# Merged branches in buffers of their own, normed x kept, two more pairs by seven products, another opening: one edit of a two-layer encoder kernel on one core

## The chip, the cores and the metric

The kernel runs on one core of a Trainium2 chip. The metric is the device time of one execution in microseconds (us). The kernel before took 1723.2, 1725.94 and 1726.93 us in three runs, median 1725.94.

The core's engines work side by side, each through its own instructions in order: TensorE (PE) multiplies matrices into PSUM, VectorE (DVE) and ScalarE (ACT) do elementwise work, GpSimd (POOL) and SyncE (SP) here mostly issue DMAs. They wait for one another by semaphores.

## The reference

Two layers of an encoder trunk over x of 512 tokens by 1024 features, all in float32. Each layer normalizes x, projects it once for four token mixers and their gates, merges the gated mixers, adds an output projection to x, and then does the feed-forward part (FFN) that the change is about:

```python
for l in range(DEPTH):
    h = rmsnorm(x, ln_mix[l])
    z = h @ w_in[l]
    ...
    merged = jnp.zeros_like(x)
    for n, o_branch in enumerate((o_mla, o_fnet, o_diff, o_hgrn)):
        gate = jax.nn.sigmoid(gate_logits[..., n * D_MODEL:(n + 1) * D_MODEL].astype(jnp.float32))
        merged = merged + gate.astype(x.dtype) * (o_branch @ w_branch[l, n])
    x = x + merged @ w_out[l]

    h2 = rmsnorm(x, ln_ffn[l])
    g_part, u_part = jnp.split(h2 @ w_gate_up[l], 2, axis=-1)
    x = x + (jax.nn.silu(g_part) * u_part) @ w_down[l]
```

with `rmsnorm(x, g) = x * rsqrt(mean(x * x) + eps) * g` over the features. The FFN is 2816 wide: 22 tiles of 128 for g and as many for u.

## The kernel before

**Tiles.** x lies in SBUF as eight tiles of 128 features by 512 tokens (`xin`, later `xm`; `x[k]` in the code). A product in float32 precision is made from three matmuls in a reduced format: each operand is split into a high part (an ACT copy, L121 or, with a gain, L125) and a low part (DVE: source minus high part, L122 or L126), and `mm3` (L141 to L143) multiplies high by high, low by high and high by low. In the profile the names say which is which: `wr_` is a weight as loaded, `wh_` and `wl_` its parts; `hh..` and `hl..` are the parts of the activations; the letters behind name the use (`hf`, `hq`, `hg`: the first projections; `o`: output projection; `fr`: the first three FFN products; `f`: the other FFN tiles; `d`: the down projection). One `gemm` over 1024 features is 24 matmuls of 512 columns. Weights come through two buffers `wr` and three each of `wh` and `wl`.

**Norm.** `prenorm` splits x times the gain without waiting for the norm, sums the squares of x on ACT and DVE (`sq`, `ss`), has PE add over the partitions with a matrix of ones (`ssx`), and makes the scale r from it: Ln and Exp on ACT (L150, L151, tile `y`), three DVE steps (L152 to L154, `ya` and `r`). The first products use x that isn't scaled and are multiplied by r behind (`gs<-fr`, `us<-fr`); meanwhile `normed` writes the normalized x into the same `hh`, `hl` buffers for the products that follow.

**Output projection.** The merged branches are split into `mh`, `ml`, which take the buffers `hh`, `hl` of the pool hp; eight products `o` follow, each added to `x[nt]`.

**FFN.** 22 pairs j of a g tile and a u tile. The string `SEVEN` says how a pair is made. An 8 is an ordinary pair, two `gemm`s of 24 matmuls (`eight`, L1150); the first three products of pairs 0 and 1 (`fr0` to `fr2`) are made before r is there. A 7 (`seven`, L1119) makes the pair from seven products of half size in place of eight, Strassen's way: 84 matmuls of 256 columns, L1066, into `fa`, `fb`, `fc`. It needs sums of weight blocks (`sums`, L1069): SP loads `s31`, a GpSimd DMA adds other blocks onto it in flight, `a22` is loaded too, DVE adds `s24`, and all are split (`vh_f`, `vl_f`, `wh_f`, `wl_f`). It also needs sums of the normalized x, made once a layer in four steps (`right_sums`, behind pairs 0 to 3): `tt` and its parts `th`, `tl`. For these the normalized tile `xn` is computed a second time (`gained`, L1034). The `fr` tiles and `fb` share two PSUM banks, and the other products share four.

After 8, 16 and 22 pairs the down projection `d` adds its part to x.

**Order.** The order of the instructions on each engine is set by a scheduler that lists them by priority, its own estimates of time, and the buffers that are free. `tc.high_priority(AHEAD)` lets a weight's loads and splits run ahead of the code around them; `keep_in_program_order` holds an instruction where it is written. At run time each engine keeps to its list. The mixers are put in order by the string `ORDER`, which isn't touched.

## Time and profile before

| | us |
|---|---|
| three runs | 1723.2, 1725.94, 1726.93 (median 1725.94) |
| profiled execution | 1724.95 |
| its span, first to last instruction | 1723.2 |
| PE busy | 1697.8 (99%) |
| DVE busy | 1179.0 (68%) |
| ACT busy | 808.8 (47%) |
| POOL busy | 43.0 (2%) |

The page gives for each group of instructions the line, engine and operation, the tiles written and read, and the count; the views of the trace give start and duration of each instruction and, in brackets, how long its engine stood idle before it and what ended that. `SPq` marks a DMA issued by SP. Matmuls are pipelined: their rows overlap, so the time of one is read from the distance between starts.

The stages in the first layer by the trace: first products from 6.6 us, output projection from 467.4, FFN from 511.9, the first pair by seven products from 579.4; in the second layer the output projection begins at 1321.3 and the FFN at 1365.8.

### The profile page before, as it was taken

The page shows a single profiled execution, that of the slowest core. Times are in us where ns is not written, and L with a number is a line of the kernel's source. Part 1 is how long each engine was busy: PE and PEld are TensorE (multiplying, and loading weights), DVE is VectorE, ACT ScalarE, POOL GpSimd, SP SyncE. Part 2 cuts the span into 40 slices and gives each one's busy share as a digit, 9 for nine tenths or more (in the row PEclk, how much of TensorE's full clock was granted, in tenths as well). Part 3 has the DMA queues.
Part 4 walks back from the last instruction along what each step waited for, and adds up shares of the span by engine and source line. Part 5 has one row for each costly group of instructions (what it writes and reads, how often), then busy time and mean ns, then how long its engine had stood idle before and what let it go on. Part 6 is the DMA issues. An engine that isn't in the chain of part 4 may idle for free.

```text
span 1723.2 us, 25722 instructions
## 1 busy us (share of the span) xinstructions
PE 1697.8 (99%) x10220; PEld 1422.5 (83%) x10220; DVE 1179.0 (68%) x1979; ACT 808.8 (47%) x1352; POOL 43.0 (2%) x68
## 2 busy tenths in 40 slices
PE   8999999999999999999999999999999999999999
PEld 6787778877787989989887777788777788899897
DVE  8858775457769647748677687754667695487473
ACT  7374353456555424525453743534564453254251
POOL 1000000000000000000000000000000000000000
PEclk9999999999999999999999999999999999999999
DMA  5222203332262435644442221142323624365443
GB/s 193 64 80 86 74 26 115 105 99 86 87 201 100 138 110 161 170 122 126 133 136 58 87 74 62 43 119 97 110 75 111 189 87 140 118 177 145 127 115 104
DMA packets 62473, 191.58 MB, mean 111 GB/s; under 512 B 7953, under 2 KB 9361, under 8 KB 62353
## 3 DMA queue, kind: packets, MB, share of 16 engines
q1 hardware_dynamic: 56304, 170.10, 30.4%
q0 software_dynamic: 5760, 19.42, 6.2%
q8 instruction: 80, 1.31, 0.3%
q10 hardware_dynamic: 288, 0.43, 0.1%
q14 instruction: 41, 0.33, 0.1%
HBM read 179.42 MB, written 4.19 MB: 107 GB/s over the span
## 4 chain that ended last, share of the span: by engine, by line
PE 87%; DVE 7%; ACT 3%; DMA 2%; issue 1%; SPq 0%; POOLq 0%; ACTq 0%; DVEq 0%
PE fb L1066 8%; PE g L142 6%; PE g L141 6%; PE g L143 6%; PE fc L1066 5%; PE fa L1066 5%; PE d L141 5%; PE d L143 5%; PE d L142 5%; PE f L142 3%; PE f L141 3%; PE f L143 3%; DMA s_f<-in_w_gu 2%; PE av L942 1%; PE sm L909 1%; PE hf L142 1%
## 5 line engine op out<-in xcount | busy, mean ns | idle before, releaser
L141 PE MATMUL g<-hhm,wh_g 128*128 128x512 f32 x512 | 202.0, 394 | 0.0
L143 PE MATMUL g<-hhm,wl_g 128*128 128x512 f32 x512 | 201.5, 394 | 0.0
L142 PE MATMUL g<-hlm,wh_g 128*128 128x512 f32 x512 | 201.5, 394 | 0.0
L143 PE MATMUL d<-ah,wl_d 128*128 128x512 f32 x352 | 136.9, 390 | 0.5 <-DVE wl_d L122 0.5
L141 PE MATMUL d<-ah,wh_d 128*128 128x512 f32 x352 | 137.2, 392 | 0.0
L142 PE MATMUL d<-al,wh_d 128*128 128x512 f32 x352 | 137.1, 390 | 0.0
L122 DVE TENSOR_TENSOR wl_g<-wr_g,wh_g 128x1024 fp32r<-128x1024 f32 x64 | 78.3, 1223 | 73.8 <-ACT wh_g L121 73.8
L121 ACT ACTIVATE wh_g<-wr_g 128x1024 fp32r<-128x1024 f32 x64 | 67.7, 1058 | 115.4 <-PE g L142 80.1
L142 PEld LDWEIGHTS g<-hlm,wh_g 128*128 128x128 f32 x512 | 96.3, 188 | 20.4 <-issue 1.5
L141 PEld LDWEIGHTS g<-hhm,wh_g 128*128 128x128 f32 x512 | 96.3, 188 | 20.2 <-issue 0.8
L143 PEld LDWEIGHTS g<-hhm,wl_g 128*128 128x128 f32 x512 | 96.3, 188 | 20.0 <-issue 0.8
L121 ACT ACTIVATE wh_d<-wr_d 128x1024 fp32r<-128x1024 f32 (+1 forms) x48 | 47.5, 989 | 111.7 <-PE d L142 85.5
L118 DVE TENSOR_TENSOR xm<-xm,d 128x512 f32<-128x512 f32 x48 | 33.0, 688 | 88.9 <-PE d L143 88.8
L121 ACT ACTIVATE wh_f<-wr_f 128x1024 fp32r<-128x1024 f32 x50 | 53.0, 1059 | 79.1 <-PE d L142 35.0
L121 ACT ACTIVATE vh_f<-s_f 128x512 fp32r<-128x512 f32 x64 | 40.1, 630 | 103.4 <-PE fb L1066 63.8
L910 DVE TENSOR_REDUCE nm<-sm 128x1 f32<-128x512 f32 x64 | 43.8, 689 | 51.3 <-PE sm L909 50.9
L143 PEld LDWEIGHTS d<-ah,wl_d 128*128 128x128 f32 x352 | 66.1, 188 | 14.9 <-DVE wl_d L122 1.4
L141 PEld LDWEIGHTS d<-ah,wh_d 128*128 128x128 f32 x352 | 66.0, 188 | 14.9 <-ACT ah L121 1.9
L142 PEld LDWEIGHTS d<-al,wh_d 128*128 128x128 f32 x352 | 66.1, 188 | 14.0 <-DVE al L122 1.2
L1066 PE MATMUL fb<-th,vh_f 128*128 128x256 f32 x256 | 75.7, 296 | 0.4 <-DVE uu L118 0.3
L1066 PE MATMUL fa<-hhf,wl_f 128*128 128x256 f32 x256 | 72.7, 284 | 0.0
L1066 PE MATMUL fa<-hlf,wh_f 128*128 128x256 f32 x256 | 72.5, 283 | 0.0
(444 smaller groups left out, 4845.6 us busy)
## 6 DMA issues: line engine op xcount, KB each, us to landing
wr_g<-in_w_g SPq DMA_DIRECT2D x64, 512.0 KB, 3.6
wr_f<-in_w_gu SPq DMA_DIRECT2D x50, 512.0 KB, 3.5
s_f<-in_w_gu SPq DMA_DIRECT2D x32, 512.0 KB, 4.5
s_f<-in_w_gu POOLq DMA_DIRECT2D x32, 512.0 KB, 5.4
wr_d<-in_w_d SPq DMA_DIRECT2D x32, 512.0 KB, 3.5
wr_b<-in_w_b SPq DMA_DIRECT2D x16, 512.0 KB, 3.4
wr_o<-in_w_o SPq DMA_DIRECT2D x16, 512.0 KB, 3.5
a_f<-in_w_gu SPq DMA_DIRECT2D x32, 256.0 KB, 3.0
```

The lines of the kernel that those rows point to most:

```text
L118: V.tensor_tensor(out, a, b, op=ALU.add)
L121: A.activation(hi, src, AF.Copy)
L122: V.tensor_tensor(lo, src, hi.bitcast(F32), op=ALU.subtract)
L141: T.matmul(ps, lh, rh, start=first, stop=False)
L142: T.matmul(ps, lh, rl, start=False, stop=False)
L143: T.matmul(ps, ll, rh, start=False, stop=last)
L909: T.matmul(ps, qs[0:96, t * P:(t + 1) * P], ks[0:96], start=True, stop=True)
L910: V.tensor_reduce(nm[:, j:j + 1], ps, axis=AX.X, op=ALU.max, negate=True)
L942: T.matmul(av[e * 64:e * 64 + 64], vv[:, b, 2 * i + e], pts[i][e][:, b].rearrange("p t q -> p (t q)"), start=t == 1 and b == 0, stop=b == ...
L1066: T.matmul(ps[:, :H], lh[:, c], rh, start=first and k == 0 and n == 0, stop=k == Q - 1 and n == 2, skip_group_check=True)
```

## The change

There are four edits.

- *Opening.* The table of gains and constants (`pk`) is loaded and ACT's function table set before anything else; PE gets ten matmuls of a 128x128 tile of ones into a PSUM tile that nobody reads; the loads of x and of the first two weights keep the written order, with the second weight (hf01) in two halves between the tiles of x.
- *Merged branches.* `mh` and `ml` lie in a pool `om` that is open from the first merged tile to the last output product, and no longer in the buffers of `hh` and `hl`.
- *Normed x.* `normed` writes each `xn[k]` into a buffer of its own (those of the later `ah4` to `ah7` and `al4` to `al7`), and `right_sums` reads it there.
- *Pairs.* `SEVEN` has four 8s in place of six: pairs 4 and 5 of each layer are made by seven products.

```diff
--- before.py
+++ after.py
@@ -29,8 +29,9 @@
 LOG_EXP = "natural_log_exp_and_others"
 WL, WR = 3, 2
 LAYERS = range(L)
-SEVEN = "8888887777777777777777"
+SEVEN = "8888777777777777777777"
 AHEAD = 156
+EARLY = 10
 ORDER = "ccbccchhhchhcbchcghcchcchzccczccbccccccchgcgccchbbbcbhcgbzcbbcbccbgghcbgcgcbcccghchghchzhbccccbccccgcccccczhgcgbgchcgcccccccggggggbgcggggbcbbggcbbcbhcccbccbccccccccccccccccccbchccgbgggbchcbbbbbbhbbb"
 PE = 8
 PM = 4
@@ -74,10 +75,17 @@
             pool("pq", 2, space=bass.MemoryType.PSUM) as pq:
 
 
+        pk0 = cp.tile([P, PK_N], F32, tag="pk", name=f"pk{LAYERS[0]}")
+        tc.keep_in_program_order(nc.scalar.dma_start(pk0, io["pk"][LAYERS[0]]))
+        tc.keep_in_program_order(nc.scalar.preload_act_table_set(LOG_EXP))
+        ones = cl.tile([P, P], F32, name="ones")
+        V.memset(ones, 1.0)
+
+        early = pq.tile([P, S], F32, tag="sc", name="early")
+        for _ in range(EARLY):
+            T.matmul(early[:, :P], ones, ones, start=True, stop=True)
         ident = cl.tile([P, P], F32, name="ident")
         make_identity(nc, ident)
-        ones = cl.tile([P, P], F32, name="ones")
-        V.memset(ones, 1.0)
         blk64 = cp.tile([P, P], F32, name="blk64")
         V.memset(blk64, 0.0)
         V.memset(blk64[0:64, 0:64], 1.0)
@@ -89,11 +97,11 @@
         xpool = [None]
         x = []
 
-        def load_x(src, who):
+        def load_x(src, who, keep=lambda i: i):
             xpool[0] = pool(f"x{who}", side="right")
             px = xpool[0].__enter__()
             x[:] = [px.tile([P, S], F32, name=f"x{who}_{k}") for k in range(KD)]
-            return [lambda k=k: nc.sync.dma_start(x[k], src[k]) for k in range(KD)]
+            return [lambda k=k: keep(nc.sync.dma_start(x[k], src[k])) for k in range(KD)]
 
         def drop_x():
             xpool[0].__exit__(None, None, None)
@@ -125,13 +133,13 @@
             A.activation(hi, src, AF.Copy, scale=g)
             V.scalar_tensor_tensor(lo, src, g, hi.bitcast(F32), op0=ALU.mult, op1=ALU.subtract)
 
-        def weight(src, n, name, cuts=(), between=None):
+        def weight(src, n, name, cuts=(), between=None, keep=lambda i: i):
             raw = rp.tile([P, 1024], F32, tag="wr", name=f"wr_{name}")
             hi = wp.tile([P, 1024], F32R, tag="wh", name=f"wh_{name}")
             lo = wp.tile([P, 1024], F32R, tag="wl", name=f"wl_{name}")
             with tc.high_priority(AHEAD):
                 for a, b in zip((0,) + cuts, cuts + (n,)):
-                    nc.sync.dma_start(raw[:, a:b], src[:, a:b])
+                    keep(nc.sync.dma_start(raw[:, a:b], src[:, a:b]))
                     split(hi[:, a:b], lo[:, a:b], raw[:, a:b])
                     if between:
                         between.pop()()
@@ -226,25 +234,31 @@
         xs = nc.dram_tensor("x_mid", (KD, P, S), F32).ap()
         for l in LAYERS:
             lam_init = 0.8 - 0.6 * math.exp(-0.3 * l)
-            pk = cp.tile([P, PK_N], F32, tag="pk", name=f"pk{l}")
-            tc.keep_in_program_order(nc.scalar.preload_act_table_set(LOG_EXP))
-            nc.scalar.dma_start(pk, io["pk"][l])
+            if l == LAYERS[0]:
+                pk = pk0
+            else:
+                pk = cp.tile([P, PK_N], F32, tag="pk", name=f"pk{l}")
+                tc.keep_in_program_order(nc.scalar.preload_act_table_set(LOG_EXP))
+                nc.scalar.dma_start(pk, io["pk"][l])
 
 
             if l == LAYERS[0]:
                 with tc.high_priority(1000):
-                    loads = load_x(io["x"], "in")
-                    w0 = weight(io["w_z"][l, 0], 1024, "hf00", (256,), [loads[1], loads[0]])
-                    for load in loads[2:]:
-                        load()
+                    loads = load_x(io["x"], "in", tc.keep_in_program_order)
+                    some = lambda *ks: lambda: [loads[k]() for k in ks]
+                    w0 = weight(io["w_z"][l, 0], 1024, "hf00", (256,), [some(1, 2, 3), some(0)],
+                                tc.keep_in_program_order)
+                    w1 = weight(io["w_z"][l, 1], 1024, "hf01", (512,), [some(6, 7), some(4, 5)],
+                                tc.keep_in_program_order)
             else:
+                w1 = None
                 w0 = weight(io["w_z"][l, 0], 1024, "hf00")
             with pool(f"mo{l}") as mo, pool(f"mx{l}") as mp:
                 hh, hl, scale, normed = prenorm(pk[:, PK_MIX:PK_MIX + 8], f"m{l}")
                 first = [gemm(None, hh, hl, "hf00", w0)]
                 r = scale()
                 for c, name in ((1, "hf01"), (4, "hq0"), (6, "hg0")):
-                    first.append(gemm(io["w_z"][l, c], hh, hl, name))
+                    first.append(gemm(io["w_z"][l, c], hh, hl, name, w1 if c == 1 else None))
                 sig0 = mp.tile([P, 3, S], F32, name="sig0")
                 for j in range(2):
                     mul(sig0[:, j], first[j], r)
@@ -366,12 +380,16 @@
                         yield gate(n, nt)
                     done.add("gates")
 
-                mh, ml = [], []
+
+                mh, ml, om = [], [], []
 
                 def merged(n):
+                    if not om:
+                        om.append(pool(f"om{l}"))
+                        om.append(om[0].__enter__())
                     for k in range(len(mh), n):
-                        h = hp.tile([P, S], F32R, tag="hh", name=f"mh{k}", bufs=KD)
-                        lo = hp.tile([P, S], F32R, tag="hl", name=f"ml{k}", bufs=KD)
+                        h = om[1].tile([P, S], F32R, name=f"mh{k}")
+                        lo = om[1].tile([P, S], F32R, name=f"ml{k}")
                         split_g(h, lo, acc[k], 0.5)
                         mh.append(h)
                         ml.append(lo)
@@ -971,7 +989,7 @@
                             if t == NT - 1:
                                 yield f"b{2 * KD - 1}"
                                 yield from normed(i)
-                        done.add(2)
+                    done.add(2)
 
                 def chain(*gens):
                     for g in gens:
@@ -1012,6 +1030,7 @@
                 for nt in range(KD):
                     ps = gemm(io["w_o"][l, nt], mh, ml, f"o{nt}", wo.get(nt))
                     add(x[nt], x[nt], ps)
+                om[0].__exit__(None, None, None)
 
 
 
@@ -1029,18 +1048,20 @@
                 def minus_sub(out, a, b):
                     V.scalar_tensor_tensor(out, a, -1.0, b, op0=ALU.mult, op1=ALU.subtract)
 
-                def gained(k, r):
-                    xn = tmp([P, S], "sq", name="xn")
-                    V.scalar_tensor_tensor(xn, x[k], pk[:, PK_FFN + k:PK_FFN + k + 1], r, op0=ALU.mult, op1=ALU.mult)
-                    return xn
+                xn = {}
 
                 def normed(r):
+
                     for k in range(KD):
-                        split(hh[k], hl[k], gained(k, r))
-
-                def right_sums(k, r):
-
-                    a, b = gained(k, r), gained(k + Q, r)
+                        own, tag = ((fa, "ah"), (fp, "al"))[k // Q]
+                        xn[k] = own.tile([P, S], F32, tag=f"{tag}{Q + k % Q}", name=f"xn{k}")
+                        V.scalar_tensor_tensor(xn[k], x[k], pk[:, PK_FFN + k:PK_FFN + k + 1], r, op0=ALU.mult,
+                                               op1=ALU.mult)
+                        split(hh[k], hl[k], xn[k])
+
+                def right_sums(k):
+
+                    a, b = xn.pop(k), xn.pop(k + Q)
                     t = fp.tile([P, 4, H], F32, tag="s24", name="tt")
                     sub(t[:, 0], a[:, :H], a[:, H:])
                     minus_sub(t[:, 1], t[:, 0], b[:, H:])
@@ -1181,7 +1202,7 @@
                     for j in range(k0, k0 + m):
                         (seven if SEVEN[j] == "7" else eight)(j)
                         if j < Q:
-                            right_sums(j, r)
+                            right_sums(j)
                     rest()
                     for nt in range(KD):
                         ps = acc_psum(f"d{nt}")
```

How this moves instructions, at three places of the first layer's FFN (the second has the same order there). Numbers behind a name tell buffers apart.

**ACT around the norm's scale**, before. `y` is Ln and then Exp for r, `wr_f` weights of ordinary tiles, `hhf<-xn` the first split of the normalized x:

```order
L121 ACTIVATE wh_fr_4916<-wr_fr_4915 128x1024
L125 ACTIVATE hhf_4816<-xm_7_4517,pk_94 128x512
L183 ACTIVATE sq<-xm_7_4517 128x512
L121 ACTIVATE wh_f_5005<-wr_f_5004 128x1024
L150 ACTIVATE y_4877<-ssx,eps 128x512
L151 ACTIVATE y_4877<-y_4877 128x512
L121 ACTIVATE wh_f_5057<-wr_f_5056 128x1024
L121 ACTIVATE hhf_4788<-xn 128x512
```

The same place in the change, where `s_f_5224` and `s_f_5326` are the sums `s31` of pairs 4 and 5:

```order
L129 ACTIVATE wh_fr_4934<-wr_fr_4933 128x1024
L133 ACTIVATE hhf_4834<-xm_7_4534,pk_79 128x512
L191 ACTIVATE sq<-xm_7_4534 128x512
L129 ACTIVATE wh_f_5019<-wr_f_5018 128x1024
L158 ACTIVATE y_4895<-ssx,eps 128x512
L129 ACTIVATE vh_f_5240<-s_f_5224 128x512
L159 ACTIVATE y_4895<-y_4895 128x512
L129 ACTIVATE vh_f_5244<-s_f_5224 128x512
L129 ACTIVATE vh_f_5248<-a_f_5226 128x512
L129 ACTIVATE vh_f_5342<-s_f_5326 128x512
L129 ACTIVATE wh_f_5067<-wr_f_5066 128x1024
L129 ACTIVATE hhf_4806<-xn_4964 128x512
```

The splits of two accumulated sums now stand between Ln and Exp and ahead of the first normalized tile; before, such splits (of pairs 6 and 7) stood in the output projection, well ahead of these rows.

**DVE behind r**, before. `gs<-fr` and `us<-fr` read the first two products out of PSUM, `hlf` are low parts of the normalized x:

```order
L154 SCALAR_TENSOR_TENSOR r<-ya,y_4877 128x512
L1034 SCALAR_TENSOR_TENSOR xn<-xm_0_4510,pk_94,r 128x512
L1034 SCALAR_TENSOR_TENSOR xn<-xm_1_4511,pk_94,r 128x512
L115 TENSOR_TENSOR gs<-fr_4849,r 128x512
L115 TENSOR_TENSOR us<-fr_4890,r 128x512
L122 TENSOR_TENSOR wl_f_5058<-wr_f_5056,wh_f_5057 128x1024
L122 TENSOR_TENSOR hlf_4789<-xn,hhf_4788 128x512
L1034 SCALAR_TENSOR_TENSOR xn<-xm_2_4512,pk_94,r 128x512
```

In the change, the stretch that ends with the same two reads (its first rows, from r to the fourth `hlf`, stand ahead of these):

```order
L130 TENSOR_TENSOR wl_f_5099<-wr_f_5097,wh_f_5098 128x1024
L130 TENSOR_TENSOR hlf_4823<-xn_4980,hhf_4822 128x512
L1058 SCALAR_TENSOR_TENSOR xn_4984<-xm_5_4532,pk_79,r 128x512
L1058 SCALAR_TENSOR_TENSOR xn_4988<-xm_6_4533,pk_79,r 128x512
L1058 SCALAR_TENSOR_TENSOR xn_4992<-xm_7_4534,pk_79,r 128x512
L130 TENSOR_TENSOR hlf_4827<-xn_4984,hhf_4826 128x512
L130 TENSOR_TENSOR hlf_4831<-xn_4988,hhf_4830 128x512
L130 TENSOR_TENSOR hlf_4835<-xn_4992,hhf_4834 128x512
L123 TENSOR_TENSOR gs<-fr_4867,r 128x512
L123 TENSOR_TENSOR us<-fr_4908,r 128x512
```

The two reads moved from behind the first two `xn` to behind the last `hlf`. PE's list changes with them: before, the matmuls of f3 and f4 alternate from the middle of f3 on; in the change f3's 24 come first and f4's first matmul waits for the read of `fr0`.

**SP's loads**, before, from the output projection on (`s_f` is the load of `s31`):

```order
L1078 DMA s_f_5362<-in_w_gu 128x1024
L134 DMA wr_o_4744<-in_w_o 128x1024
L1080 DMA a_f_5364<-in_w_gu 128x512
L1078 DMA s_f_5464<-in_w_gu 128x1024
L1080 DMA a_f_5466<-in_w_gu 128x512
L134 DMA wr_fr_4843<-in_w_gu 128x1024
L1080 DMA a_f_5888<-in_w_gu 128x512
L134 DMA wr_fr_4884<-in_w_gu 128x1024
L134 DMA wr_fr_4915<-in_w_gu 128x1024
L134 DMA wr_f_5004<-in_w_gu 128x1024
L134 DMA wr_f_5056<-in_w_gu 128x1024
```

In the change:

```order
L142 DMA wr_o_4761<-in_w_o 128x1024
L142 DMA wr_fr_4861<-in_w_gu 128x1024
L142 DMA wr_fr_4902<-in_w_gu 128x1024
L142 DMA wr_fr_4933<-in_w_gu 128x1024
L142 DMA wr_f_5018<-in_w_gu 128x1024
L1099 DMA s_f_5224<-in_w_gu 128x1024
L1101 DMA a_f_5226<-in_w_gu 128x512
L142 DMA wr_f_5066<-in_w_gu 128x1024
L1099 DMA s_f_5326<-in_w_gu 128x1024
L1101 DMA a_f_5328<-in_w_gu 128x512
L142 DMA wr_f_5097<-in_w_gu 128x1024
```

The first two loads of `s31` moved from ahead of the last `wr_o` and the `wr_fr` to behind `wr_f3` (`wr_f_5018`) and `wr_f4` (`wr_f_5066`).

## The prediction

> **What bounds the kernel now.** I read the page's busy times and its chain first. TensorE (PE) is busy for 99% of the span and carries most of the chain that ends last.
>
> ```profile
> span 1723.2 us, 25722 instructions
> PE 1697.8 (99%) x10220; PEld 1422.5 (83%) x10220; DVE 1179.0 (68%) x1979; ACT 808.8 (47%) x1352; POOL 43.0 (2%) x68
> PE 87%; DVE 7%; ACT 3%; DMA 2%; issue 1%; SPq 0%; POOLq 0%; ACTq 0%; DVEq 0%
> ```
>
> So time is won only by giving PE fewer matmuls, by running them at a higher clock, or by closing one of PE's few waits; and any new wait of PE costs its full length. The table of PE's waits shows how little there is to close:
>
> ```profile
> PE hf L141 <- ACT hhm L125: 6.6, 1, 6.6
> PE fo L143 <- DVE ab L122: 1.9, 2, 1.0
> PE ssx L188 <- DVE ss L118: 1.2, 2, 0.7
> ```
>
> The profiled execution took 1724.95 us; its span is 1723.2, and 1.75 lie outside. The sum below is made against it. The median of the runs, 1725.94, lies 0.99 above.
>
> **The opening.** The rows of ScalarE (ACT) and PE at the start, in order of start, duration and what is done:
>
> ```profile
> 1.20 1.28 ACT L86 ACT_TABLE_LOAD   x1 [1.20 <-PEq L1298]
> 4.09 0.42 ACT L121 ACTIVATE wh_hf<-wr_hf 128x256 fp32r<-128x256 f32 x1 [1.29 <-DMA wr_hf<-in_w_z]
> 4.53 1.28 ACT L230 ACT_TABLE_LOAD   x1
> 5.82 0.72 ACT L125 ACTIVATE hhm<-xin,pk 128x512 fp32r<-128x512 f32 x1
> 11.90 0.71 ACT L125 ACTIVATE hhm<-xin,pk 128x512 fp32r<-128x512 f32 x1
> 6.59 0.79 PE L141 MATMUL hf<-hhm,wh_hf 128*128 128x512 f32 x1 [6.59 <-ACT hhm L125]
> 12.56 0.63 PE L141 MATMUL hf<-hhm,wh_hf 128*128 128x512 f32 x1
> 12.99 0.59 PE L142 MATMUL hf<-hlm,wh_hf 128*128 128x512 f32 x1
> 13.65 0.39 PE L141 MATMUL hf<-hhm,wh_hf 128*128 128x512 f32 x1
> 13.87 0.39 PE L142 MATMUL hf<-hlm,wh_hf 128*128 128x512 f32 x1
> 22.25 0.39 PE L141 MATMUL hq<-hhm,wh_hq 128*128 128x512 f32 x1
> ```
>
> Two things cost time. The first matmul waits behind a second table load (4.53, 1.28 us) between the weight's split and the first `hhm`. And matmuls start 0.43 us apart (12.56 to 12.99) until about 13.4, then 0.22 (13.65 to 13.87): for 6.8 us PE ran at half rate. The change loads the table once, before anything waits for it; the first `hhm` can then follow the split at 4.5, when `x[0]` has landed, and the first product starts near 5.7, 0.9 us earlier. It also gives PE ten small matmuls on `ones` from about 1.1 us. They are a quarter of a 512-column matmul each, in plain F32; I estimate 0.43 us each, 4.3 in all, from the pitch above and the two-pass `ssx` (below: x2 for one product), so they end before the product could start.
>
> If full rate comes 6.8 us after 1.1, that is at 7.9 us, some dozen half-rate matmuls at 0.2 us excess go away: 2.4 us more. But the cover is thin: the loads are now written as x[0..3], half of hf01's weights, x[4], x[5], the other half, x[6], x[7], so the last `x` comes after 512 KB more than before. The last `hhm` was split at 11.90; behind these loads I put its end at 14.0 instead of 12.6, its low part at 15.1, and what is left of the two products after that lets `hq` start at 19.2 at the best, 3.05 earlier than 22.25. The bounds are 0.9 (clock as before) and 3.05; I take **-2.0**, since a later `hq` also still has `ssx` inside it.
>
> The Trainium skill (TensorE: Matmul & The Clock Gate, Part 1: The HAM clock gate) says that the half rate is the default and that a busy window of about 3.4 us releases it. The rows show 6.8 us between the first product and full rate, twice that. By the page the ten early matmuls would release it before the first product, and the opening would give the 3.05.
>
> **The merged branches.** `mh` and `ml` get their own buffers, so the FFN's `hhf`, `hlf` no longer wait for the last output product to let go of them. Before, six of the eight `hhf` were done in one block, and the sum of squares and PE followed late:
>
> ```profile
> 509.34 3.78 ACT L125 ACTIVATE hhf<-xm,pk 128x512 fp32r<-128x512 f32 x6
> 516.50 1.49 DVE L118 TENSOR_TENSOR ss<-ss,sq 128x512 f32<-128x512 f32 x2
> 517.09 0.39 PE L143 MATMUL fr<-hhf,wl_fr 128*128 128x512 f32 x1
> 518.05 1.13 PE L188 MATMUL ssx<-ss,ones 128*128 128x512 f32 x2 [0.57 <-DVE ss L118]
> 1372.11 1.12 PE L188 MATMUL ssx<-ss,ones 128*128 128x512 f32 x2 [0.68 <-DVE ss L118]
> ```
>
> With the splits spread behind each `x[k]`, the sum is ready before 517.3. One matmul's pitch after 517.09 is 517.32, so 0.73 us go there; with the second layer's, **-1.5**. If the cover goes, nothing is lost over now.
>
> **Two more pairs a layer by seven products.** An ordinary pair is 48 matmuls of 512 columns; a seven-product pair is 84 of 256. Here is PE on tile f, as start and end of a window, its length and busy time; then the first matmul after the second pair of sevens, and tile d in their window:
>
> ```profile
> 530.00:579.39 49.39, 49.34 (x216) 1.00 0.36 111
> 579.39 0.28 PE L1066 MATMUL fa<-hhf,wh_f 128*128 128x256 f32 x1
> 601.21 0.40 PE L141 MATMUL d<-ah,wh_d 128*128 128x512 f32 x1
> 579.39:601.21 21.82, 1.55 (x6) 1.00 0.49 142
> ```
>
> 216 matmuls in 49.39 us are 0.2287 each, 10.98 a pair. From 579.39 to 601.21 PE did two sevens and six `d` matmuls (6 x 0.227 = 1.4): 10.2 a pair. 0.76 less for each of four pairs: **-3.0**. DVE pays for it: beside PE it has room later (below), but not here.
>
> **Normed x kept.** Eight scalar_tensor_tensor a layer go, 0.75 us each from the two at 522.77 (x2, 1.41) to single ones: 6 us of DVE. PE did not wait for them, so I cost the edit at nothing by itself; it lightens the stretch of the next part.
>
> **What the moved order adds.** With pairs 4 and 5 now sevens, their sums of weights come two pairs (22 us) earlier: `s31` is loaded, then a GpSimd DMA adds onto it, then ACT splits it (`vh_f`). SP's order now has the loads of `s31` behind `wr_f3`, where they were in the output product before. And ACT's order puts `vh_f` of pair 4 between Ln and Exp of the norm's `r`, and `vh_f` of pair 5 ahead of the first `hhf` of the normed `x`. ACT works in order: all eight `hhf` now queue behind two accumulating DMAs. On DVE all eight `hlf` stand ahead of `gs<-fr0`, whose reading of `fr0` frees the PSUM bank that f4's first matmul needs; before, that multiply came right behind the first two `xn`. What such an accumulate takes, from the issue of its load, the trace shows:
>
> ```profile
> 482.97 0.38 SPq L1078 DMA_DIRECT2D s_f<-in_w_gu  x1
> 499.13 1.15 ACT L121 ACTIVATE vh_f<-s_f 128x512 fp32r<-128x512 f32 x2 [7.40 <-DMA s_f<-in_w_gu]
> s_f<-in_w_gu SPq DMA_DIRECT2D x32, 512.0 KB, 4.5
> s_f<-in_w_gu POOLq DMA_DIRECT2D x32, 512.0 KB, 5.4
> 488.89 0.89 POOL L1081 DMA_DIRECT2D s_f<-in_w_gu  x1 [259.64 <-DMA s_f<-in_w_gu]
> ```
>
> In the loaded stretch it was 499.1 - 483.0 = 16.1 us; with both medians and 0.6 from landing to issue it is 4.5 + 0.6 + 5.4 = 10.5. ACT lost 7.40 us there, which cost PE nothing, since no PE work hung on it. Now it does. The rows around:
>
> ```profile
> 509.59 17.55 SPq L134 DMA_DIRECT2D wr_f<-in_w_gu  x4
> 514.71 1.23 DVE L122 TENSOR_TENSOR wl_fr<-wr_fr,wh_fr 128x1024 fp32r<-128x1024 f32 x1
> 522.05 0.69 DVE L154 SCALAR_TENSOR_TENSOR r<-ya,y 128x512 f32<-128x512 f32 x1
> 522.77 1.41 DVE L1034 SCALAR_TENSOR_TENSOR xn<-xm,pk,r 128x512 f32<-128x512 f32 x2
> 538.61 0.69 DVE L122 TENSOR_TENSOR hlf<-xn,hhf 128x512 fp32r<-128x512 f32 x1
> 539.21 0.43 DVE L1027 TENSOR_TENSOR tt<-xn 128x256 f32<-128x256 f32 x1
> 529.93 0.39 PE L141 MATMUL f<-hhf,wh_f 128*128 128x512 f32 x1
> 520.00:540.00 20.00, 19.95 (x88) 15.95 (x87) 19.09 (x29) 10.26 (x15) 0.00 (x0) 1.00 0.22 79
> 540.00:560.00 20.00, 20.00 (x90) 16.58 (x89) 19.61 (x31) 10.91 (x13) 0.00 (x0) 1.00 0.32 110
> ```
>
> (In the last two, the busy time of PE, weight loads, DVE and ACT.) I follow the first layer on before's clock. `wr_f4` has a buffer when `wl_fr2` is split, 515.9 before (514.71 + 1.23), and I put it 1.6 earlier in the new order, where its high part no longer stands behind the block of six `hhf`: s31 of pair 5 is issued behind it at 514.35. With 12.4 us, nearer the medians than the worst because half as many loads run there, its accumulate lands at T5 = 526.75. From T5 ACT does `vh_f` (0.6), the split of f4's weights (1.0) and the first `hhf` (0.6); DVE then has in order eight `hlf` (0.60 each: 538.61 to 539.21, while the row itself says 0.69), six `xn` (0.68), one 1024-wide low part (1.23 less the same 0.09) and `gs` (0.60), 10.6 us. `gs<-fr0` is done at T5 + 13.0 = 539.75. f4 could have started at 529.93 - 0.73 + 24 x 0.227 = 534.65. PE stands for **5.1 us**, in f3 (whose matmuls follow each `hlf`) and before f4. Before, the last `hlf` was just as late (538.61), but f4's matmuls ran between f3's, so nothing was lost.
>
> The bounds: T5 = 524.85 by the medians gives 3.2; 16.1 us gives 530.45 and 8.8. Were both accumulates early, r would be ready at 522.0 plus up to 1.5 for the three `vl_f` now between its steps, and 13.15 of DVE (with the first two `xn` and one low part) ends at 535.2 to 536.7: 0.5 to 2.0. Layer 1 has the same order on all three queues: twice 5.1, **+10.2**.
>
> The first sevens then want their `tl`, `s24` and `wl` while DVE, full at 19.6 of 20 us already, has nine-odd us of splits for each seven in place of four. Bounds 0 and 2.0 a layer; half a microsecond is nearest to a DVE that was relieved of 6: **+1.0**.
>
> **The sum.** -2.0 - 1.5 - 3.0 + 10.2 + 1.0 = +4.7: 1724.95 + 4.7 = 1729.7, and with the median's 0.99 1730.6. I say **1730 us**.
>
> **The rivals.**
>
> *The accumulates land in time.* For it: quiet ones take 10.5 us or less, and r is needed only at 522. Then the stall is 0.5 to 2.0 a layer: -6.5 + 2.5 + 0.5 = -3.5, about 1721.5, and with the best opening 1719. Against it: for pair 5 even the medians give 524.85, later than r. Chance 0.34.
>
> *PE falls back to half rate while f3 waits.* PE is less than half busy for some 11 us. A return to 0.43 us would add 0.2 to each of about 16 matmuls behind it, as the opening's rows show: 3.2 a layer, 1736. Decisive only if gaps in f3 are long; they are about 0.6 each, the length of a `hlf`. Chance 0.08.
>
> *The opening gives nothing.* The later `x` eats what the clock gives, 0.9 or less stays: 1731. For it: `hhm` of x[7] really is later. Chance 0.08 with the main stall in place.
>
> *My forecast*: 0.50, with its own range from 1725 to 1736.
>
> **How the numbers follow.** A measurement here tells 0.2%, about 3.5 us, from no change. Of the first rival's 0.34, 0.24 lie below 1722.5 and 0.10 within; of the forecast's 0.50, 0.06 below (stalls of 1 us, full opening), 0.09 within and 0.35 above; of the last two 0.01, 0.02 and 0.13. Faster 0.31, same 0.21, slower 0.48. The range 1718 to 1738 holds the first rival and stalls up to 8.8 in one layer.
>
> **What would show it.** Right: an ACT row of `vh_f` between the two `y` with a wait on the DMA s_f of 1 us or more, another before `hhf`, and a wait of PE on DVE at f4 (`gs`) near 540, twice about 5 us; `ssx` without a wait on `ss`; `hq` starting near 20. Wrong: no PE wait at f4; full rate not before 13.4; sevens of 11 us each because PE waits on `wl_f` or `uu`.

## The result, and the profile after

The changed kernel took 1738.89 us (median of four runs, 1738.64 to 1739.16), beside 1724.86 us for the kernel before on the same chip: a ratio of 1.0081, with its 95% interval [1.0063, 1.0098]. It is 14.0 us slower. The forecast was 1730 us, 5 slower, with a range up to 1738: the sign was right, the size was not.

The page of the changed kernel, as quoted of before: span, busy times, chain.

```profile
span 1737.1 us, 26104 instructions
PE 1705.4 (98%) x10384; PEld 1433.3 (83%) x10384; DVE 1188.5 (68%) x2004; ACT 816.2 (47%) x1372; POOL 46.6 (3%) x72
PE 84%; DVE 8%; ACT 3%; DMA 3%; issue 1%; SPq 0%; DVEq 0%; ACTq 0%; POOLq 0%
```

PE's share of the chain fell by three points, and DVE and DMA have two of them. The table of PE's waits says where (total, times, longest):

```profile
PE f L150 <- DVE hlf L130: 6.2, 8, 1.1
PE f L149 <- ACT hhf L129: 4.2, 6, 1.2
PE fc L1087 <- DVE us L126: 2.4, 2, 1.4
PE hf L149 <- ACT hhm L133: 1.8, 1, 1.8
```

The wait of `ssx` on `ss` is gone, as forecast. In its place stand fourteen waits in f3, in two layers, for the split of the normalized x, and one in the first sevens of each layer.

The table gives when the first matmul of each stage began, in the profiled execution of both kernels (us from the start of the span):

| stage begins | before | after | moved by |
|---|---|---|---|
| hq | 22.25 | 21.56 | -0.69 |
| hg | 27.69 | 27.91 | +0.22 |
| o, layer 0 | 467.39 | 468.32 | +0.93 |
| ssx, layer 0 | 518.05 | 518.25 | +0.20 |
| f3, layer 0 | 529.93 | 531.42 | +1.49 |
| first seven, layer 0 | 579.39 | 564.83 | -14.56; with two ordinary pairs (21.96) fewer ahead of it, +7.40 |
| d, layer 0 | 596.84 | 605.24 | +8.40 |
| o, layer 1 | 1321.27 | 1329.37 | +8.10 |
| ssx, layer 1 | 1372.11 | 1379.27 | +7.16 |
| f3, layer 1 | 1384.00 | 1391.90 | +7.90 |
| first seven, layer 1 | 1433.45 | 1425.10 | -8.35; likewise +13.61 |
| d, layer 1 | 1450.90 | 1465.14 | +14.24 |
| end of the span | 1723.2 | 1737.1 | +13.9 |

Set against the terms of the prediction, with the differences of layers 0 and 1 in brackets:

| term | predicted | measured |
|---|---|---|
| opening | -2.0 | +0.93 (up to o) |
| ssx | -1.5 | -1.67 (0.20 - 0.93, 7.16 - 8.10) |
| wait in f3 and f4 | +10.2 | +13.65 (7.40 - 0.20, 13.61 - 7.16) |
| four pairs by sevens, matmuls alone | -3.0 | -3.0 (by the pitches of before: 20.46 in place of 21.96 a layer) |
| waits in the first sevens | +1.0 | +4.6 (40.41 and 40.04 from first seven to d, where 17.45 + 20.46 = 37.91 was to be expected) |
| rest | 0 | -0.6 |
| sum | +4.7 | +13.9 |

The two great terms can be read row by row. ACT of the changed kernel around the norm's scale; the brackets give its idle time and what ended it:

```profile
519.31 0.69 ACT L158 ACTIVATE y<-ssx,eps 128x512 f32<-128x512 f32 x1
525.38 0.63 ACT L129 ACTIVATE vh_f<-s_f 128x512 fp32r<-128x512 f32 x1 [5.38 <-DMA s_f<-in_w_gu]
525.92 0.62 ACT L159 ACTIVATE y<-y 128x512 f32<-128x512 f32 x1
529.27 0.63 ACT L129 ACTIVATE vh_f<-s_f 128x512 fp32r<-128x512 f32 x1 [1.70 <-DMA s_f<-in_w_gu]
530.76 1.16 ACT L129 ACTIVATE hhf<-xn 128x512 fp32r<-128x512 f32 x2
```

Between Ln and Exp ACT stood 5.38 us for the first accumulated sum, and 1.70 more for the second, ahead of the first `hhf`. DVE, PE and the DMAs of the same stretch:

```profile
529.06 0.68 DVE L162 SCALAR_TENSOR_TENSOR r<-ya,y 128x512 f32<-128x512 f32 x1
540.36 1.89 DVE L130 TENSOR_TENSOR hlf<-xn,hhf 128x512 fp32r<-128x512 f32 x3
542.17 0.69 DVE L123 TENSOR_TENSOR gs<-fr,r 128x512 f32<-128x512 f32 x1
531.42 0.50 PE L149 MATMUL f<-hhf,wh_f 128*128 128x512 f32 x1 [1.22 <-ACT hhf L129]
541.11 0.50 PE L150 MATMUL f<-hlf,wh_f 128*128 128x512 f32 x1 [0.76 <-DVE hlf L130]
515.51 0.42 SPq L1099 DMA_DIRECT2D s_f<-in_w_gu  x1
521.67 0.88 POOL L1102 DMA_DIRECT2D s_f<-in_w_gu  x1 [5.30 <-DMA s_f<-in_w_gu]
```

r is there 7 us later than before (529.06, before 522.05). The second sum was loaded from 515.51, added to from 521.67 and there at 529.27: 13.8 us.

### The profile page after: what moved, and what is told of

The parts are those of the page before. It is cut to its first block, busy times and chain, and to the rows that moved or that the text cites. A ratio compares the mean times of both kernels' runs of the same rounds, so it can differ in the third digit from the quotient of the medians.

```text
span 1737.1 us, 26104 instructions
## 1 busy us (share of the span) xinstructions
PE 1705.4 (98%) x10384; PEld 1433.3 (83%) x10384; DVE 1188.5 (68%) x2004; ACT 816.2 (47%) x1372; POOL 46.6 (3%) x72
## 4 chain that ended last, share of the span: by engine, by line
PE 84%; DVE 8%; ACT 3%; DMA 3%; issue 1%; SPq 0%; DVEq 0%; ACTq 0%; POOLq 0%
PE fb L1087 9%; PE g L150 6%; PE g L149 6%; PE g L151 6%; PE fc L1087 6%; PE fa L1087 5%; PE d L149 5%; PE d L151 5%; PE d L150 5%; DMA s_f<-in_w_gu 2%; PE f L150 2%; PE f L149 2%; PE f L151 2%; PE o L150 1%; PE o L151 1%; PE o L149 1%
## 5 line engine op out<-in xcount | busy, mean ns | idle before, releaser
L129 ACT ACTIVATE vh_f<-s_f 128x512 fp32r<-128x512 f32 x72 | 45.3, 629 | 110.1 <-PE fb L1087 72.2
L1087 PE MATMUL fb<-th,vh_f 128*128 128x256 f32 x288 | 84.9, 295 | 0.1
L1087 PE MATMUL fa<-hhf,wh_f 128*128 128x256 f32 x288 | 81.6, 283 | 0.4 <-ACT wh_f L129 0.4
L1087 PE MATMUL fa<-hhf,wl_f 128*128 128x256 f32 x288 | 81.7, 284 | 0.0
L1087 PE MATMUL fa<-hlf,wh_f 128*128 128x256 f32 x288 | 81.5, 283 | 0.0
L1087 PE MATMUL fb<-th,vl_f 128*128 128x256 f32 x288 | 81.4, 283 | 0.0
L1087 PE MATMUL fb<-tl,vh_f 128*128 128x256 f32 x288 | 81.3, 282 | 0.0
L129 ACT ACTIVATE wh_f<-wr_f 128x1024 fp32r<-128x1024 f32 x46 | 48.6, 1057 | 68.7 <-PE d L150 35.0
```

What stands on the lines that cost most here:

```text
L129: A.activation(hi, src, AF.Copy)
L1087: T.matmul(ps[:, :H], lh[:, c], rh, start=first and k == 0 and n == 0, stop=k == Q - 1 and n == 2, skip_group_check=True)
```

## The experiments

Two theories stood against each other on what had moved the splits `vh_f` to that place. *Pairs*: as the prediction said, making pairs 4 and 5 by sevens brings their sums there. *Own buffers*: the buffers of the merged branches do, because the FFN's buffers would be given out behind them. Two runs take one of the two away.

**Six ordinary pairs in the changed kernel.**

```diff
-SEVEN = "8888777777777777777777"
+SEVEN = "8888887777777777777777"
```

> The changed kernel with six ordinary pairs again, all else kept. Theory 'own buffers': the order that puts the splits of two accumulated sums between Ln and Exp and ahead of the normalized tiles comes from the buffers of the merged branches, so the wait of f3 and f4 (7.2 and 6.4 us in the changed kernel) stays; the 3.0 us that four sevens save go, and so do the 4.6 us that PE lost inside the first sevens: about 1737 us. Theory 'pairs' (the prediction's): pairs 4 and 5 as sevens brought the loads of s31 to that place; with six pairs the wait goes: about 1725 us.

Measured: 1738.85 us (ratio to before 1.0085 [1.0058, 1.0112]), as slow as with four. The splits of pair 6 now stand at the same place, and from the start of f3 to the first seven PE took 56.85 and 54.95 us, where before took 49.46 and 49.45. (These are from its profiled execution of 1742.21 us, in which PE's clock was also halved for 10.2 us of f3 and f4 in layer 0.) Theory *pairs* falls.

**Own buffers alone, on the kernel before.**

```diff
-                mh, ml = [], []
+                mh, ml, om = [], [], []
...
+                    if not om:
+                        om.append(pool(f"om{l}"))
+                        om.append(om[0].__enter__())
...
-                        h = hp.tile([P, S], F32R, tag="hh", name=f"mh{k}", bufs=KD)
-                        lo = hp.tile([P, S], F32R, tag="hl", name=f"ml{k}", bufs=KD)
+                        h = om[1].tile([P, S], F32R, name=f"mh{k}")
+                        lo = om[1].tile([P, S], F32R, name=f"ml{k}")
...
+                om[0].__exit__(None, None, None)
```

> The kernel before with the merged branches in buffers of their own, nothing else. Theory 'own buffers': ACT stands for the sum s31 of pair 6 ahead of Exp, r is some 6 us late, and PE stands in f3, less what the alternation of f3 and f4 still hides: 1730 to 1737 us, with ssx no longer waiting (-1.6). Theory 'pairs': only the wait of ssx goes: 1723.3 us.

Measured: 1736.06 us (1.0061 [1.0038, 1.0084]). This edit alone costs 11 us. ACT's rows are those of the changed kernel:

```profile
518.13 0.69 ACT L150 ACTIVATE y<-ssx,eps 128x512 f32<-128x512 f32 x1
523.84 0.63 ACT L121 ACTIVATE vh_f<-s_f 128x512 fp32r<-128x512 f32 x1 [5.02 <-DMA s_f<-in_w_gu]
524.38 0.62 ACT L151 ACTIVATE y<-y 128x512 f32<-128x512 f32 x1
528.24 0.63 ACT L121 ACTIVATE vh_f<-s_f 128x512 fp32r<-128x512 f32 x1 [2.20 <-DMA s_f<-in_w_gu]
```

**The other way round: kept x and four pairs without own buffers**, on the kernel before (and so with its opening).

```diff
-SEVEN = "8888887777777777777777"
+SEVEN = "8888777777777777777777"
...
-                        split(hh[k], hl[k], gained(k, r))
+                        own, tag = ((fa, "ah"), (fp, "al"))[k // Q]
+                        xn[k] = own.tile([P, S], F32, tag=f"{tag}{Q + k % Q}", name=f"xn{k}")
...
+                        split(hh[k], hl[k], xn[k])
...
```

(`right_sums` reads the kept tiles, as in the change.)

> The kernel before with the normed x kept and four ordinary pairs; merged branches and opening as before. Theory 'own buffers': the sums of pairs 4 and 5 are loaded and split inside the output projection, r is there at 522, f3 and f4 lose at most 1 us a layer; the sevens save 3.0 and lose what DVE cannot give them at their start, 0 to 2.5 us a layer: 1722 to 1727 us. Theory 'pairs': the wait for the accumulating DMA is there as in the changed kernel: 1735 us or more.

Measured: 1726.2 us (1.0007 [0.9997, 1.0017]). The wait for the sums is where it was before, in the output projection, and Exp follows Ln:

```profile
499.82 1.16 ACT L121 ACTIVATE vh_f<-s_f 128x512 fp32r<-128x512 f32 x2 [8.06 <-DMA s_f<-in_w_gu]
519.93 0.69 ACT L150 ACTIVATE y<-ssx,eps 128x512 f32<-128x512 f32 x1 [0.97 <-PE ssx L188]
520.66 0.63 ACT L151 ACTIVATE y<-y 128x512 f32<-128x512 f32 x1
```

So theory *own buffers* holds: own buffers alone bring the wait, and without them it is not there. By what way they move the sums (the FFN's buffers given out later) was not tried apart. But the 3.0 us of the four pairs are not there either. By the same stages as in the table above it lost, beside before, 0.7 and 0.3 us ahead of `ssx`, 0.6 in each layer from f3 to the first seven, and 1.55 and 0.74 from the first seven to `d`.

**Only the place of the splits.** In the changed kernel the splits of `s31` and `a22` are listed on ACT behind the last `hhf` of the normalized x:

```diff
+                        with tc.issue_after(behind[0].ins):
+                            v1 = pair(s31[:, 512:], 512)
+                            v3 = pair(s31[:, :512], 512)
+                            v22 = pair(a22, 512)
```

(`behind[0]` is the last `hhf` that `normed` issues; the three lines stood there without the `with`.)

> The changed kernel, with the splits of s31 and a22 (vh_f) listed on ACT behind the last split of the normalized x; nothing else. If the accumulating DMA ahead of Exp and hhf is what costs, r is there at about 522 us as before, the wait of PE in f3 and f4 falls from 7.2 and 6.4 us to 0 to 2, and the time to 1726 to 1729 us. If DVE is the bound there (all hlf ahead of the read of fr0), 2 to 3 us a layer stay and it is 1731 to 1733 us.

Measured: 1729.45 us (1726.24 to 1732.25; 1.0024 [1.0007, 1.0041]), 9.4 less than the changed kernel and just above the range expected. From f3 to the first seven PE now took 28.07 and 28.04 us, 0.6 over what its matmuls need; the wait of 7.2 and 6.5 us is gone. This shows the cause of the greatest term: the two accumulating DMAs ahead of r and `hhf`. (With them out of the way the scheduler also set the read of `fr0` ahead of the last `hlf`, and five of f4's matmuls ahead of f3's last two; the run with own buffers alone has that read further ahead still and lost 3.6 us and more.) But from the first seven to `d` it was 44.17 and 43.54 us, 6.3 and 5.6 over the expected 37.91. The rows of the first sevens (DVE, SP, POOL, ACT, PE):

```profile
558.53 0.69 DVE L126 TENSOR_TENSOR s_f<-s_f,wr_f 128x512 f32<-128x512 f32 x1
559.25 0.33 SPq L1101 DMA_DIRECT2D s_f<-in_w_gu  x1
562.97 0.87 POOL L1104 DMA_DIRECT2D s_f<-in_w_gu  x1 [42.59 <-DMA s_f<-in_w_gu]
571.69 1.15 ACT L129 ACTIVATE vh_f<-s_f 128x512 fp32r<-128x512 f32 x2 [4.62 <-DMA s_f<-in_w_gu]
574.03 0.39 PE L1089 MATMUL fc<-hhf,wh_f 128*128 128x256 f32 x1 [3.06 <-DVE us L126]
570.00:580.00 10.00, 6.95 (x46) 6.74 (x45) 6.65 (x11) 3.68 (x6) 1.45 (x2) 0.83 0.68 172
```

`s31` has two buffers. The load for pair 6 (559.25) had to wait until DVE made `s24` of pair 4 from the first (558.53), which comes only when the ordinary pairs are almost past and DVE has time. Load and accumulate then took 12.4 us, ACT stood for them, and PE stood 3.06 us for a `us` queued behind them on DVE. In the window that the last row shows, PE was busy 6.95 of 10 us, and its granted clock 0.83. With six ordinary pairs the first sums are needed 22 us later, and the runs with six took 17.45 us there, as before did.

**A higher place for the read of fr0.** On the kernel with kept x and four pairs, the multiplies out of PSUM get priority:

```diff
-                            mul(t[i], raw[2 * j + i], r)
+                            with tc.high_priority(AHEAD):
+                                mul(t[i], raw[2 * j + i], r)
```

> As the run with normed x kept and four ordinary pairs on the kernel before, and the multiplies that read fr0 to fr2 out of PSUM at a higher priority, so that gs<-fr0 stands right behind r on DVE. If the place of that read costs PE time in f3 and f4, this is up to 1 us a layer less than its neighbour; if the alternation of f3 and f4 hides it already, the two are equal within 0.5 us.

Measured: 1727.72 us (1.0014 [1.0004, 1.0024]), 1.5 more than its neighbour, and the expectation missed. The 0.6 us a layer between f3 and the first seven did go (27.53 and 27.50, what the matmuls need). But the first sevens of layer 0 lost 5.2 us in place of 1.55 (in layer 1 0.8 in place of 0.74), in a wait of `fb` on `wh_f` and a half-rate stretch behind it:

```profile
564.29 0.39 PE L1068 MATMUL fb<-th,wh_f 128*128 128x256 f32 x1 [1.60 <-ACT wh_f L121]
```

What DVE and ACT do earlier in f3, they do later for the first sevens. That this order is the reason was not tried apart.

**Own buffers without the wait.** The kernel before, with the three edits shown above: own buffers, kept x, the splits listed behind; six ordinary pairs.

> The kernel before with merged branches in own buffers and normed x kept, six ordinary pairs, and the splits of s31 and a22 listed behind the last split of the normalized x. Nothing waits for an accumulating DMA ahead of r, and pair 6 comes 50 us later, so its sums are there: the gain of ssx (1.6 us) is kept, f3 and f4 lose up to 0.6 us a layer: 1723 to 1724.5 us. If own buffers cost anything besides the place of vh_f, it is 1728 us or more.

Measured: 1723.69 us (0.9994 [0.9984, 1.0004]). The profiled execution lost 1.3 us in its opening; from o to d, layer 0 gained 0.47 on before and layer 1 0.63: `ssx` brought 0.75 and 0.91, and the stretch behind f3 gave 0.4 back. So own buffers cost nothing that this time shows, once `vh_f` stands elsewhere.

**One more pair by sevens, five ordinary ones**, on the same kernel.

```diff
-SEVEN = "8888887777777777777777"
+SEVEN = "8888877777777777777777"
```

> Own buffers, kept x, the splits behind, the old opening, and five ordinary pairs in place of six. One more seven a layer saves 1.5 us in all. If the start of the sevens is bound by how early their sums are split (DVE and ACT are full until the ordinary pairs are past), PE loses that again in waits of fc and fb: 1723 to 1725 us. If only pair 4 came too early, 1722 us.

Measured: 1722.15 us (0.9988 [0.9979, 0.9998]). From the first seven to `d` it took 27.78 us in both layers, where 17.45 + 10.23 = 27.68 is all that the matmuls need. The 0.75 us a layer of pair 5 is kept; what the runs with four ordinary pairs lose comes with pair 4.

**The opening of before in the changed kernel.** The core of it, the rest likewise as before:

```diff
-        early = pq.tile([P, S], F32, tag="sc", name="early")
-        for _ in range(EARLY):
-            T.matmul(early[:, :P], ones, ones, start=True, stop=True)
...
-                    w0 = weight(io["w_z"][l, 0], 1024, "hf00", (256,), [some(1, 2, 3), some(0)],
-                                tc.keep_in_program_order)
...
+                    w0 = weight(io["w_z"][l, 0], 1024, "hf00", (256,), [loads[1], loads[0]])
```

> The changed kernel with the opening of the kernel before. The changed opening cost 0.87 us up to the output projection, half-rate stretches of PE at 9.9 to 13.3 us and 64.5 to 71.3 us among it. If these come from the opening, the second is gone with it and the time is 0.9 us less, about 1738.0 us. If the second has another cause (the mixers' own gaps), it stays and the time is 1739 us or more.

Measured: 1737.57 us (1.0071 [1.0048, 1.0094]), 1.3 less than the changed kernel. Up to the output projection it was 1.13 us behind the kernel before, where the changed kernel was 0.93 behind: the half-rate stretch near 64.5 stayed, so it comes without the new opening too. The time nevertheless fits the 1738.0 of the other theory, and that is luck: it comes from the sevens of layer 1, which took 38.54 us to `d` in place of 40.04. (The diff also moves the line `done.add(2)` out of a loop. This run keeps that, and up to the output projection its PE, DVE and SP do the same work in the same order as before, so that line moved nothing there.)

**The opening alone, and without its ten matmuls.**

> The kernel before with the changed opening alone. Theory 'full queues': the first 3 MB fill the DMA engines until about 13 us whatever their order, the last x comes later, and PE starts earlier only to wait: the beginning of hg moves by -1.0 to +0.6 us (as in the three runs with this opening so far: -0.99, +0.14, +0.63) and the time is 1724 to 1726 us. Theory of the prediction: early matmuls bring the full clock and 2 us: 1722.8 us.

> The kernel before with the changed opening but without the ten matmuls on ones. If these matmuls are what raises the clock at 5 to 7 us, full rate now comes about two windows of 3.4 us after the first product, near 12 to 13 us, and hq starts up to 1.2 us later than with them. If the clock falls back anyway while PE waits for x, hq starts within 0.3 us of the run with them.

The second leaves out the loop of ten matmuls on `ones` and its PSUM tile; these compute nothing that is used. Measured: 1723.7 us (0.9991 [0.9982, 1.0]) and 1723.73 us (0.9996 [0.9987, 1.0005]). They can't be told apart, and `hq` began at 20.94 and 20.91 us. The first time lies 0.3 us under the range of theory *full queues* and 0.9 above the other's figure; `hg` moved by -0.40. (The shifts that the expectation names for the three earlier runs are -0.83, +0.22 and +0.68 by the table's reading.) PE with the ten matmuls, then without, by three windows (length, PE busy, granted clock, DMA share, GB/s):

```profile
2.90:6.50 3.60, 3.44 (x16) 1.00 1.00 351
6.50:9.90 3.40, 1.86 (x5) 0.91 1.04 384
9.90:13.30 3.40, 3.40 (x10) 0.58 1.00 385
```

```profile
2.90:6.50 3.60, 0.65 (x1) 1.00 0.98 354
6.50:9.90 3.40, 3.00 (x6) 1.00 1.04 382
9.90:13.30 3.40, 3.40 (x10) 1.00 1.03 399
```

In both, ten matmuls fit into the third window; in both they start 0.43 us apart until about 12.6, so the 1.00 of the second kernel there isn't a full clock (the column seems to count the time ahead of the first change as full). With the ten matmuls the clock was full in most of the second window, 0.91, but PE had 1.86 us of work in it: the DMA engines were full until 13.3 and `x[1]` was on its way. In the third window the clock was back at 0.58. So theory *full queues* holds for the ten matmuls. The rest of the new opening (table first, order of loads) is worth about 0.7 us by the medians, which the second interval doesn't tell from nothing.

**Own buffers, kept x, splits behind, with the changed opening.**

> Own buffers, kept x, the splits of s31 behind the last split of the normalized x, six ordinary pairs, and the changed opening. If the opening is worth nothing, as its sibling with the old opening, 1723 to 1724 us; with the best opening seen (-1.0) 1722.5 us; with the worst 1724.5 us.

Measured: 1723.98 us (0.9994 [0.9985, 1.0003]), no difference from its sibling with the old opening.

**What was left standing, together**: own buffers, kept x, splits behind, five ordinary pairs, the opening without its matmuls.

> What the runs left standing, together: own buffers, kept x, the splits of s31 behind the last split of the normalized x, five ordinary pairs, and the changed opening without its ten matmuls. If the parts add up: 0.7 us (the opening alone against the kernel before) less than the same kernel with the old opening, 1722.15, so 1721.5 us, faster than the kernel before by 0.15 to 0.2%. If the opening's spread from run to run eats its gain: 1722.2 us.

Measured: 1721.99 us (1721.11 to 1723.28), a ratio of 0.9985 [0.9976, 0.9994]. This version is faster than both kernels, by 2.6 us than before and 17 than the change. The opening adds nothing to the 1722.15 of the run without it.

## Why the prediction was right or wrong

**Right: the sign, and what ACT waits for.** Of the rows asked for these are there: `vh_f` between the two `y` with a wait on the accumulating DMA, another ahead of `hhf`, PE standing in f3, and `ssx` without its wait. The forecast chain was T5, then 13.0 us to the read of fr0; measured, 529.27, then 13.6 to 542.86. The run that moved only these splits removed the wait, which shows it.

**Wrong: PE's wait at f4.** The prediction asked for "a wait of PE on DVE at f4 (`gs`) near 540, twice about 5 us" and called its absence a sign of being wrong. It is absent. All of PE's idle time there lies in f3, in layer 0 2.4 us on `hhf` and 3.2 on `hlf`, and f4's first matmul follows f3's last at the usual pitch:

```profile
542.83 0.39 PE L151 MATMUL f<-hhf,wl_f 128*128 128x512 f32 x1
543.06 0.40 PE L149 MATMUL f<-hhf,wh_f 128*128 128x512 f32 x1
```

The read of fr0 ended at 542.86. So f3 itself, held by the late splits, ended when the read did, and a sum by the read comes to the same time; what the read alone would cost these rows don't show.

**Mis-sized: the wait.** The step "With 12.4 us, nearer the medians than the worst" put T5 at 526.75. The issue of the load was 515.51, not 514.35, and load and accumulate took 13.8 us. Hence 7.2 and 6.5 us a layer, inside the bounds of 3.2 and 8.8, where 5.1 was taken: 3.5 us of the miss.

**Wrong: what caused it.** "With pairs 4 and 5 now sevens, their sums of weights come two pairs (22 us) earlier" read the order rightly and its cause wrongly. Own buffers alone bring the sums there, whichever pair is first. I had set the row of the order beside the edit that named pairs 4 and 5 and asked no further. So the edit that I credited with -1.5 was the one that cost most. The sum didn't suffer from that, since all edits came together; a forecast for each edit would have.

**Wrong: the opening, by 2.9 us.** The step "If full rate comes 6.8 us after 1.1 ... some dozen half-rate matmuls ... go away" took full rate, once there, to stay. In the changed kernel's execution it was there from 6.5 to 9.9 us and then went, while PE stood 1.79 us for `x[1]`:

```profile
8.99 0.50 PE L149 MATMUL hf<-hhm,wh_hf 128*128 128x512 f32 x1 [1.79 <-ACT hhm L133]
```

```profile
6.50:9.90 3.40, 1.32 (x4) 1.00 1.05 393
9.90:13.30 3.40, 3.40 (x8) 0.51 1.00 372
```

The section of the Trainium skill that I had set beside it (TensorE: Matmul & The Clock Gate, Part 1: The HAM clock gate) has the other half of the rule too: an idle window of about 3.4 us brings the half rate back. I had used only the first half. The trace goes further than that rule: PE was busy for 1.32 us of the window from 6.50 to 9.90, not idle, and the clock fell all the same. It went so in all five traces with the ten matmuls: by the granted clock full rate came at 5.1 to 7.2 us, went 3.4 us later and was back at 11.9 to 14.0. In the nine traces without them it came at 10.4 to 13.5; the 6.8 us from the first product to full rate, on which the step rests, was one execution's figure, and with the old opening it was anything from 3.9 to 6.8.

Of the 2.9 us, 1.7 were missing when `fn` began (-0.32 us beside before, where -2.0 was forecast). Another 1.7 went in the half-rate stretch near 64.5, up to the next stage, `cq` (+1.39), and 0.5 came back by `o`. The stretch stands in three of the seven traces with the new opening and in one of the seven with the old, so it doesn't need the new opening; whether that helps to bring it is not shown. The +0.93 itself is within the scatter: `o` began at 466.2 to 468.9 us in the seven traces with the new opening (mean 467.6) and at 466.9 to 468.7 with the old (467.7). No trace has the -2.0.

**Mis-sized: the first sevens**, +1.0 forecast and +4.6 measured. The step "half a microsecond is nearest to a DVE that was relieved of 6" saw DVE's work, and not what its order hangs on: the two buffers of `s31`, the next accumulate behind them, and ACT and DVE standing for it. The changed kernel has a milder form of what the run with the moved splits showed. The load for pair 6 was issued at 567.32, its sum was there at 578.01, and PE stood for a `us` listed behind it on DVE:

```profile
578.01 0.63 ACT L129 ACTIVATE vh_f<-s_f 128x512 fp32r<-128x512 f32 x1 [2.60 <-DMA s_f<-in_w_gu]
580.36 0.39 PE L1087 MATMUL fc<-hhf,wh_f 128*128 128x256 f32 x1 [1.05 <-DVE us L126]
```

PE was idle for 3.15 of the 4.6 us (busy 38.81 of 40.41 us and 38.49 of 40.04). No run took the buffers of `s31` or this accumulate away alone, so the reason is read from the rows. The saving of the matmuls, 0.75 a pair, was as forecast. Of the 3.0 us for two pairs more, 2.3 to 11.9 are lost there in the five runs that have them; for one pair more it is kept.

**The rivals.** "The accumulates land in time" did not happen. (Its 1719 with the best opening is a slip: 1721.5 less the 1.05 between -2.0 and -3.05 is 1720.4.) "PE falls back to half rate while f3 waits" did not happen in the profiled execution of the changed kernel, but it did in those with own buffers alone (below), with six pairs and with the old opening. Its price was taken as 3.2 us a layer. In the run with the old opening PE's clock was halved for 6.8 us of f3 in layer 0, and from `ssx` to the first seven it took 47.04 us where the changed kernel took 46.58: there the half rate fell into time in which PE waited anyway. "The opening gives nothing" held, as a part beside the forecast.

## What to carry to other kernels

Where a scheduler writes the order, an edit to buffers can move work of another stage: read the order with each edit alone before a cause is named, and look on each in-order engine for an instruction that waits on a DMA ahead of a short chain that everything needs (here Exp and the first splits of the normalized x). A cheaper form of a product is worth its matmuls only from the point where its inputs can be ready: here one pair earlier was kept whole, and with two pairs earlier most of the gain, or more than all of it, was lost. Matmuls that only raise the clock bought nothing here, where real work couldn't follow at once.

## What the hardware showed beyond that

PE's clock fell to half in stretches of 3.4 or 6.8 us though PE was never idle for long. Windows of the changed kernel, and the first two windows of f3 in the run with own buffers alone:

```profile
61.10:64.50 3.40, 2.85 (x43) 1.00 0.44 141
64.50:67.90 3.40, 3.28 (x42) 0.51 0.05 18
67.90:71.30 3.40, 3.40 (x34) 0.50 0.00 0
```

```profile
527.80:531.20 3.40, 1.73 (x7) 1.00 0.23 77
531.20:534.60 3.40, 2.87 (x6) 0.53 0.44 154
```

The stretch near 64.5 came in some kernels and not in others with the same matmuls there (not in before, where PE was busy 3.05 us from 61.10 to 64.50 against 2.85 here), and in the opening's run alone it came at 917.3 in the second layer instead. It cost 1.7 us here (from `fn` to `cq` 22.23 in place of 20.51 us), as much as most edits here are worth. What decides it stays open: no run changed it alone.

The same loads do not land alike either. With the same opening, ACT began the split of `x[1]` at 8.22 us in the changed kernel, 1.20 us after it was free, and at 7.00 in the run with the splits moved, where `hq` began 1.05 us earlier (20.51 against 21.56). The edits between them lie 500 us later.
